# A state space branch with y and z on feature partitions, heads paired on halves of the array's columns

## The chip, the core and the metric

The kernel runs on one core of one Trainium2 chip. The metric is device time in microseconds (us) for one execution; lower is better. TensorE (PE in the rows) multiplies matrices, with its weight loads shown apart as PEld; VectorE (DVE) and ScalarE (ACT) do elementwise work, GpSimd (POOL) a few small operations, SyncE (SP) issues the DMAs. L with a number is a line of the kernel file: of the kernel before, if nothing else is said.

## The reference

Two layers of a trunk with three branches (differential attention, latent attention "MLA", and a state space branch), a gated merge and a feed-forward network, all in float32 on 512 tokens of width 1024. The change is in the state space branch. Cut to it:

```
xs, bm, cm = split(silu(causal_conv(xbc)))         # 16 heads of 64, 4 groups, state 128
dt = softplus(dt_raw + bias);  a = -exp(a_log)
# chunks of L = 128 tokens, 4 heads share a group's bm and cm
cs = cumsum(dt * a) over the chunk
decay = exp(cs[l] - cs[s]) where s <= l
y_diag = (cm[l] . bm[s] * decay) @ (xs * dt)
states = bm^T @ (xs * dt * exp(cs_end - cs));  prev = scan over chunks
y_off  = (cm @ prev) * exp(cs)
ys = (y_diag + y_off + d * xs) * silu(z)
ys = ys * rsqrt(mean(ys^2 over the group's 256 features) + eps) * ssm_norm
merged += sigmoid(gate_c) * (ys @ w_branch_c)
```

## The kernel before

**Products.** Every float32 product is made of three float32r passes: an operand is split into a high and a low part (`wh`/`wl` for weights, `hh`/`hl` for the normed input, `yh`/`yl` for a branch's result), and high x high, low x high and high x low are summed in PSUM. `mm3` (L144 to L147) issues the three. `lin_feat` (`feat_groups`) makes a product with features on partitions: per group of 256 columns two PSUM banks `mb` of 128x512, in two halves of 24 matmuls of 512 moving columns. `lin_tok` (`tok_groups`, L224 to L226) makes one with tokens on partitions: per group of 256 columns 96 matmuls of 256 moving columns. Before each half, `split` turns a loaded 128x1024 tile `wr` into `wh` (ScalarE, L140) and `wl` (VectorE, L141); three such pairs are in flight. What is plain float32 (transposes, the products inside the branch) is issued by TensorE as two instructions per matmul, except transposes.

**The branch.** `mix` runs the state space branch first, in four groups g of four heads. A group has three products: x and (b, c), each followed by a causal convolution of the bank (`conv`: one ScalarE pass L877, three VectorE taps L879 into a tile `u`, a tanh L883 and a multiply L884 into `cv`), and z. Then, on float32 operands:

- x (two 128-row tiles `cv[0]`, `cv[1]`) is transposed to tokens (L914); VectorE makes `xdt` (L918) and starts `y` with d times x (L920). b is transposed (L926), c.b is formed (L931) and masked (`cb`, L933); `xte` (L938), the states (L944) and `prev` (L946 to L951) follow.
- For each of four heads a matmul with `sel` spreads the running sum over 512 columns (L957), VectorE takes a minimum (L959), ScalarE four exponentials of 128x128 (L962), VectorE multiplies by `cb` (L963), and four matmuls with `dec` as weights and 64 columns of `xdt` moving (L965) give y with tokens on partitions.
- Three matmuls of 256 columns (L971) give the part from earlier chunks, which VectorE scales and adds (L973, L976); L968 adds the first part, L977 multiplies by silu(z).
- ScalarE sums the squares per token (L981), GpSimd takes the power -0.5 (L110).
- The `tail` of a group is issued inside the next group's products: VectorE scales y (L986), TensorE transposes it back to features (eight transposes, L990), ScalarE and VectorE split it into `yh` and `yl` (L993, L994).

After the fourth group come the gate products of the merge and its tail, then the MLA attention: its first products (L1082, L1104), VectorE's norms of them (L1088 to L1116, with four powers on GpSimd), and the transposes of `qn` and `kn` (L1123).

**What sets the order.** A scheduler lays out the instructions of each engine up to the attention; from there on TensorE's order is the one in which the code is written, and between its steps `fill` puts whole passes of waiting products (`MLA_HEAD` gives 5.737 and 2.613 us of them around the first transposes). Each engine works its queue in order, so an instruction that waits holds all that stand behind it. PSUM has four banks `mb` and four `ab`.

Of the kernel before, what the change touches and what calls it, by code (L numbers as in the profile page):

```python
# [9 lines left out]
F32 = mybir.dt.float32  # L10
# [8 lines left out]
P = 128  # L19
# [46 lines left out]
def trunk_kernel(ctx: ExitStack, tc: tile.TileContext, a: dict, out: bass.AP):  # L66
# [679 lines left out]
    def mix(l, x, hh, hl, ckr, cq, latp, scope):  # L746
# [79 lines left out]
        scratch = ssd.tile([P, 256], F32, name="yo", bufs=2).rearrange("p (i t h) -> p i t h", i=4, t=T)  # L826
# [15 lines left out]
        nc.vector.tensor_tensor(out=da, in0=dt, in1=rv["a"].unsqueeze(1).broadcast_to([P, T, SSM_H]), op=ALU.mult)  # L842
        zeros = ssd.tile([P, S], F32, name="cb")
# [3 lines left out]
        cs, ncs, tot, ecs, te = (ssd.tile([P, T, SSM_H], F32, name=nm) for nm in ("cs", "ncs", "tot", "ecs", "te"))  # L847

        def decays():

            cp = abank()
            daf = da.rearrange("p t h -> p (t h)")
            nc.tensor.matmul(cp[:, 0:n16], tri, daf, start=True, stop=True)
            nc.tensor.matmul(cp[:, n16:2 * n16], ones, daf, start=True, stop=True)
            ct = abank()
            for c in range(T):
                nc.tensor.matmul(ct[0:SSM_H, c * P:(c + 1) * P], da[:, c], tri, start=True, stop=True)
            nc.scalar.activation(cs_r[0:SSM_H], ct[0:SSM_H], AF.Copy)
            nc.vector.tensor_tensor(out=cs_r[32:32 + SSM_H], in0=ct[0:SSM_H], in1=cs_r[0:SSM_H], op=ALU.subtract)
# [3 lines left out]
            nc.scalar.activation(ecs.rearrange(flat), cp[:, 0:n16], AF.Exp)  # L863
# [6 lines left out]
        with ssd_scope:  # L870
            tails = []
            for g in range(SSM_G):
# [28 lines left out]
                sz = sp.tile([P, T, 256], F32, name="sz", bufs=2)  # L901

                def ev_z(tt, bank):
                    o = sz[:, 2 * tt:2 * tt + 2]
# [5 lines left out]
                y = sp.tile([P, T, 256], F32, name="y")  # L910
                for i in range(2):
                    tp = abank()
                    for c in range(T):
                        nc.tensor.transpose(out=tp[:, c * P:(c + 1) * P], in_=cv[i][:, c * P:(c + 1) * P], identity=ident)  # L914
                    tv = tp.rearrange("p (c r d) -> p c r d", c=T, r=2)
                    hs = slice(4 * g + 2 * i, 4 * g + 2 * i + 2)
                    sl = slice(i * P, (i + 1) * P)
                    nc.vector.tensor_tensor(out=xdt[:, :, sl].rearrange("p c (r d) -> p c r d", r=2), in0=tv,  # L918
                                            in1=dt[:, :, hs].unsqueeze(3).broadcast_to([P, T, 2, SSM_HD]), op=ALU.mult)
                    nc.vector.tensor_tensor(out=y[:, :, sl].rearrange("p c (r d) -> p c r d", r=2), in0=tv,  # L920
                                            in1=rv["dvec"][:, hs].unsqueeze(1).unsqueeze(3).broadcast_to([P, T, 2, SSM_HD]),
                                            op=ALU.mult)
# [30 lines left out]
                yps = [abank().rearrange("p (c d) -> p c d", c=2) for _ in range(2)]  # L953
                for r in range(4):
                    h = 4 * g + r
                    lp_ = abank()
                    nc.tensor.matmul(lp_, sel[:, h:h + 1].broadcast_to([P, P]), cs_r, start=True, stop=True)  # L957
                    dec = sp.tile([P, T, P], F32, name="dec", bufs=3)
                    nc.vector.tensor_tensor(out=dec, in0=lp_.rearrange("p (c l) -> p c l", c=T),  # L959
                                            in1=cs[:, :, h:h + 1].broadcast_to([P, T, P]), op=ALU.min)  # L960
                    for c in range(T):
                        nc.scalar.activation(dec[:, c], dec[:, c], AF.Exp, bias=ncs[:, c, h:h + 1])  # L962
                    nc.vector.tensor_tensor(out=dec, in0=dec, in1=cb.rearrange("p (c d) -> p c d", c=T), op=ALU.mult)  # L963
                    for c in range(T):
                        nc.tensor.matmul(yps[c // 2][:, c % 2, r * SSM_HD:(r + 1) * SSM_HD], dec[:, c],  # L965
                                         xdt[:, c, r * SSM_HD:(r + 1) * SSM_HD], start=True, stop=True)
                for i in range(2):
                    nc.vector.tensor_tensor(out=y[:, 2 * i:2 * i + 2], in0=y[:, 2 * i:2 * i + 2], in1=yps[i], op=ALU.add)  # L968
                for c in range(1, T):
                    op_ = abank()  # L970
                    nc.tensor.matmul(op_[:, 0:256], cmT[:, c * P:(c + 1) * P], prev[:, c - 1], start=True, stop=True)  # L971
                    yo = sp.tile([P, 256], F32, name="yo", bufs=2)
                    nc.vector.tensor_tensor(out=yo.rearrange("p (r d) -> p r d", r=4),  # L973
                                            in0=op_[:, 0:256].rearrange("p (r d) -> p r d", r=4),
                                            in1=ecs[:, c, hd].unsqueeze(2).broadcast_to([P, 4, SSM_HD]), op=ALU.mult)
                    nc.vector.tensor_tensor(out=y[:, c], in0=y[:, c], in1=yo, op=ALU.add)  # L976
# [611 lines left out]
```

## Time and profile before

| | us |
|---|---|
| median of 3 runs | 2073.7 (2073.63 to 2075.88) |
| the profiled execution, its own time | 2072.72 |
| its span, first to last instruction | 2071.0 |
| TensorE busy in the span | 2043.1 |
| VectorE busy | 1418.6 |
| ScalarE busy | 913.8 |

The mean granted TensorE clock of the span is 0.996 of full speed. A matmul's row shows its whole time through the array; matmuls overlap, so what one costs is the distance from its start to the next one's start. The chain that ended last is 87% TensorE.

### The profile page before, as it was taken

Reading aid. Unit: us, or ns where it says so; the run is one execution under the profiler, and the core shown is the slowest. Engines: PE = TensorE matmul, PEld = TensorE weight load, DVE = VectorE, ACT = ScalarE, POOL = GpSimd, SP = SyncE. Lnnn points to the kernel's source line nnn. Section 1 sums busy time; section 2 is a strip of 40 time slices with the busy share of each in tenths; the row PEclk is TensorE's granted clock in tenths of the full one; section 3 lists DMA queues with packets and bytes.
Section 4 is the critical chain, followed back from the end, with each engine's and each line's share of the span. In section 5 each row is a group of like instructions: output and inputs, shape, how many; then the busy total and the mean of one; then the engine's idle time right before and its main releaser. Section 6 shows DMA issues by size and latency. Waiting matters only on the chain.

```text
span 2071.0 us, 30143 instructions
## 1 busy us (share of the span) xinstructions
PE 2043.1 (99%) x11469; PEld 1769.7 (85%) x11469; DVE 1418.6 (68%) x2742; ACT 913.8 (44%) x1683; POOL 137.1 (7%) x162
## 2 busy tenths in 40 slices
PE   8999999999999999999999999999999999999999
PEld 7888987789888988888898888888998898888888
DVE  7788887756876678658757888775566566553553
ACT  6744445535533454224434544454444335432441
POOL 4200011002100000000000000110020000000000
PEclk8999999999999999999999999999999999999999
DMA  8523232233445255655443223212333243323222
GB/s 268 150 69 85 78 116 90 87 108 113 152 153 169 94 187 165 196 179 166 153 141 85 79 62 89 64 48 79 93 93 93 92 133 92 102 92 102 92 92 82
DMA packets 224542, 237.20 MB, mean 115 GB/s; under 512 B 16126, under 2 KB 195742, under 8 KB 224142
## 3 DMA queue, kind: packets, MB, share of 16 engines
q1 hardware_dynamic: 221646, 232.63, 36.3%
q0 software_dynamic: 2752, 2.65, 0.5%
q8 instruction: 90, 1.47, 0.3%
q14 instruction: 54, 0.44, 0.1%
HBM read 226.30 MB, written 8.91 MB: 114 GB/s over the span
## 4 chain that ended last, share of the span: by engine, by line
PE 87%; DVE 7%; DMA 2%; POOL 2%; issue 2%; ACT 1%; SPq 0%; POOLq 0%; DVEq 0%; ACTq 0%
PE mb L145 22%; PE mb L147 21%; PE mb L146 21%; PE mb L224 3%; PE mb L226 3%; PE mb L225 3%; PE ab L965 1%; DVE wl L141 1%; PE mb L666 1%; PE ab L1140 1%; PE ab L1177 1%; DVE macc L522 1%; PE ab L1326 1%; PE ab L1082 1%; POOL r_r L110 1%
## 5 line engine op out<-in xcount | busy, mean ns | idle before, releaser
L145 PE MATMUL mb<-hh,wh 128*128 128x512 f32 (+1 forms) x1376 | 538.2, 392 | 1.8 <-DVE g L778 0.9
L147 PE MATMUL mb<-hh,wl 128*128 128x512 f32 (+1 forms) x1376 | 532.4, 387 | 0.0
L146 PE MATMUL mb<-hl,wh 128*128 128x512 f32 (+1 forms) x1376 | 531.3, 386 | 0.0
L141 DVE TENSOR_TENSOR wl<-wr,wh 128x1024 fp32r<-128x1024 f32 (+2 forms) x312 | 374.9, 1203 | 193.8 <-ACT wh L140 192.5
L140 ACT ACTIVATE wh<-wr 128x1024 fp32r<-128x1024 f32 (+2 forms) x312 | 324.7, 1042 | 338.4 <-PE mb L146 260.5
L147 PEld LDWEIGHTS mb<-hh,wl 128*128 128x128 f32 x1376 | 258.4, 188 | 51.7
L145 PEld LDWEIGHTS mb<-hh,wh 128*128 128x128 f32 x1376 | 258.3, 188 | 51.8 <-DVE g L778 1.8
L146 PEld LDWEIGHTS mb<-hl,wh 128*128 128x128 f32 x1376 | 258.8, 188 | 49.1 <-DVE hl L702 1.2
L1423 DVE SCALAR_TENSOR_TENSOR fu<-mb,vec,fu 128x510 f32<-128x510 f32 (+1 forms) x176 | 129.8, 745 | 90.5 <-ACT fu L1421 88.9
L224 PE MATMUL mb<-wh,hh 128*128 128x256 f32 x640 | 180.1, 281 | 0.0
L226 PE MATMUL mb<-wh,hl 128*128 128x256 f32 x640 | 178.6, 279 | 0.0
L225 PE MATMUL mb<-wl,hh 128*128 128x256 f32 x640 | 178.5, 279 | 0.0
L145 PE MATMUL mb<-gh,wh 128*128 128x512 f32 (+1 forms) x432 | 151.2, 350 | 0.0
L147 PE MATMUL mb<-gh,wl 128*128 128x512 f32 (+1 forms) x432 | 150.6, 349 | 0.0
L146 PE MATMUL mb<-gl,wh 128*128 128x512 f32 (+1 forms) x432 | 150.5, 348 | 0.0
L1421 ACT ACTIVATE fu<-mb,vec 128x512 f32<-128x512 f32 x88 | 67.9, 774 | 149.7 <-PE mb L147 149.7
L224 PEld LDWEIGHTS mb<-wh,hh 128*128 128x128 f32 x640 | 120.0, 188 | 1.2 <-ACT wh L140 0.4
L225 PEld LDWEIGHTS mb<-wl,hh 128*128 128x128 f32 x640 | 120.1, 188 | 0.4
L226 PEld LDWEIGHTS mb<-wh,hl 128*128 128x128 f32 x640 | 120.2, 188 | 0.0
L522 DVE SCALAR_TENSOR_TENSOR macc<-wg,c_act,macc 128x512 f32<-128x512 f32 x140 | 104.6, 747 | 20.0 <-DMA wg<-in_ada_w_dram 19.2
L145 PE MATMUL mb<-yh,wh 128*128 128x512 f32 x256 | 104.5, 408 | 0.9 <-ACT g L769 0.9
L147 PE MATMUL mb<-yh,wl 128*128 128x512 f32 x256 | 100.3, 392 | 0.0
(333 smaller groups left out, 3373.9 us busy)
## 6 DMA issues: line engine op xcount, KB each, us to landing
wr<-in_w_in_dram SPq DMA_DIRECT2D x88, 512.0 KB
wr<-in_ffn_w_up_dram SPq DMA_DIRECT2D x88, 512.0 KB
wg<-in_ada_w_dram SPq DMA_DIRECT2D x160, 256.0 KB
wr<-in_ffn_w_down_dram SPq DMA_DIRECT2D x40, 512.0 KB
wr<-in_w_in_dram SPq DMA_DIRECT2D x64, 256.0 KB
wm<-in_ada_w_dram SPq DMA_DIRECT2D x16, 512.0 KB
wr<-in_w_branch_c_dram SPq DMA_DIRECT2D x16, 512.0 KB
wr<-in_w_out_dram SPq DMA_DIRECT2D x16, 512.0 KB
```

The lines of the kernel that those rows point to most:

```text
L110: nc.gpsimd.tensor_tensor(out=r, in0=ms, in1=nhalf[:, 0:1].broadcast_to([P, n]), op=ALU.pow)
L140: nc.scalar.activation(hi, raw[:, 0:n], AF.Copy)
L141: nc.vector.tensor_tensor(out=lo, in0=raw[:, 0:n], in1=hi, op=ALU.subtract)
L145: nc.tensor.matmul(o, lh, rh, start=first, stop=False)
L146: nc.tensor.matmul(o, lh, rl, start=False, stop=False)
L147: nc.tensor.matmul(o, ll, rh, start=False, stop=last)
L224: nc.tensor.matmul(o, hh[:, kk, ts_], wh[:, sl], start=first and k == 0, stop=False)
L225: nc.tensor.matmul(o, hh[:, kk, ts_], wl[:, sl], start=False, stop=False)
L226: nc.tensor.matmul(o, hl[:, kk, ts_], wh[:, sl], start=False, stop=last and k == 3)
L522: ins = nc.vector.scalar_tensor_tensor(out=acc[0], in0=rk, scalar=c_act[:, kk:kk + 1], in1=acc[0], op0=ALU.mult, op1=ALU.add)
L1421: nc.scalar.activation(u, bank, AF.Identity, bias=v[:, V_FCB + ti:V_FCB + ti + 1], scale=tap(2))
L1423: nc.vector.scalar_tensor_tensor(out=u[:, s_:], in0=bank[:, 0:S - s_], scalar=tap(2 - s_), in1=u[:, s_:], op0=ALU.mult, op1=ALU.add)
```

## The change

In each group z and y lie with features on partitions.

- z is made by `lin_feat` like x (48 matmuls of 512 columns), into `sz` of [128, 2, 512], one buffer.
- Two heads share a tile: for a pair, `dec` is [128, 2, 512] and one VectorE pass of 1024 elements multiplies both heads by `cb`. `xdt` (64 columns of a head) is now the weight, `dec` moves with 128 columns, and the two heads of a pair write the two halves of the output's partitions. `prev` is the weight of the earlier chunks' part: three matmuls of 128 columns per pair.
- The decay exp(cs) of that part comes from the spread running sum by ScalarE (64x384 per head, into `grow`); the tile `ecs` goes. d times x is folded into the pass that adds the product (`dcol` holds d as a column).
- The squares (ScalarE) of the two tiles are added (VectorE), and the `tail` sums them over all partitions with one float32 matmul of `ones` by 512 columns. ScalarE takes a square root, VectorE its reciprocal on 128x512, two passes scale y, and the split follows without transposes. The power on GpSimd goes.

```
-                lin_tok(w_in, [(C_Z + 256 * g, 256)], hh, hl, ev_z)
+                lin_feat(w_in, (C_Z + 256 * g, C_Z + 256 * g + P), KT, h_rhs, ev_z)
...
+                for i in range(2):
+                    dec = sp.tile([P, 2, S], F32, name="dec", bufs=2)
+                    grow = sp.tile([P, S], F32, name="yo", bufs=2)
+                    for r in range(2):
+                        h = 4 * g + 2 * i + r
+                        own = slice(r * SSM_HD, (r + 1) * SSM_HD)
+                        lp_ = abank()
+                        nc.tensor.matmul(lp_, sel[:, h:h + 1].broadcast_to([P, P]), cs_r, start=True, stop=True)
...
+                        nc.scalar.activation(grow[own, P:S], lp_[own, P:S], AF.Exp)
+                        for c in range(T):
+                            nc.scalar.activation(dec[:, r, c * P:(c + 1) * P], dec[:, r, c * P:(c + 1) * P], AF.Exp, bias=ncs[:, c, h:h + 1])
+                    nc.vector.tensor_tensor(out=dec, in0=dec, in1=cb.unsqueeze(1).broadcast_to([P, 2, S]), op=ALU.mult)
+                    yp = abank()
                     for c in range(T):
...
+                            nc.tensor.matmul(yp[own, cs_], xdt[:, c, i * P + r * SSM_HD:i * P + (r + 1) * SSM_HD], dec[:, r, cs_],
+                                             start=True, stop=True)
...
+                        nc.tensor.matmul(op_[:, cs_], prev[:, c - 1, i * P:(i + 1) * P], cmT[:, cs_], start=True, stop=True)
+                    nc.vector.tensor_tensor(out=grow[:, P:S], in0=grow[:, P:S], in1=op_[:, P:S], op=ALU.mult)
+                    j = 2 * g + i
+                    nc.vector.scalar_tensor_tensor(out=y[:, i], in0=cv[i], scalar=dcol[:, j:j + 1], in1=yp, op0=ALU.mult, op1=ALU.add)
+                    nc.vector.tensor_tensor(out=y[:, i, P:S], in0=y[:, i, P:S], in1=grow[:, P:S], op=ALU.add)
+                nc.vector.scalar_tensor_tensor(out=y, in0=y, scalar=0.5, in1=sz, op0=ALU.mult, op1=ALU.mult)
...
+                    nc.scalar.activation(sq[i], y[:, i], AF.Square, scale=1.0 / 16)
+                nc.vector.tensor_tensor(out=sq[0], in0=sq[0], in1=sq[1], op=ALU.add)
+                def tail(g=g, y=y, sq=sq[0]):
+                    ssp = abank()
+                    nc.tensor.matmul(ssp, ones, sq, start=True, stop=True)
+                    rows_ = sp.tile([P, S], F32, name="u", bufs=3)
+                    nc.scalar.activation(rows_, ssp, AF.Sqrt, bias=eps_)
+                    nc.vector.reciprocal(out=rows_, in_=rows_)
                     for i in range(2):
...
+                        nc.vector.scalar_tensor_tensor(out=y[:, i], in0=y[:, i], scalar=cw, in1=rows_, op0=ALU.mult, op1=ALU.mult)
                         yh, yl = y_tiles()
...
+                        nc.scalar.activation(yh, y[:, i], AF.Copy)
+                        nc.vector.tensor_tensor(out=yl, in0=y[:, i], in1=yh, op=ALU.subtract)
```

The change moves instructions on all engines of this stage. Three places follow; the changed kernel's lines are numbered a little higher (L921 is L914 of before, L929 L926, L934 L931, L947 L944, L886 and L891 the convolution's L879 and L884, L913 the z evacuation L906, L923 `xdt`, L1053 to L1133 the attention's L1043 to L1123).

First, VectorE in the last group of layer 0, from the products of z and of the taps of (b, c) to `xte`. Before:

```order
L879 SCALAR_TENSOR_TENSOR u<-mb,vec_89,u 128x509
L141 TENSOR_TENSOR wl<-wr,wh 128x1024
L884 SCALAR_TENSOR_TENSOR cv<-cv,u 128x512
L906 SCALAR_TENSOR_TENSOR sz<-sz,mb 128x512
L918 TENSOR_TENSOR xdt<-ab,dt 128x4x128
L906 SCALAR_TENSOR_TENSOR sz<-sz,mb 128x512
L920 TENSOR_TENSOR y<-ab,dvec 128x4x128
```

Now (the two rows of L891 are `cv[2]`, which is b, and `cv[3]`, which is c):

```order
L998 RECIPROCAL u<-u 128x512
L886 SCALAR_TENSOR_TENSOR u<-mb,vec_89,u 128x511
L1001 SCALAR_TENSOR_TENSOR y<-y,vec_89,u 128x512 x2
L886 SCALAR_TENSOR_TENSOR u<-mb,vec_89,u 128x510
L1004 TENSOR_TENSOR yl<-y,yh 128x512 x2
L886 SCALAR_TENSOR_TENSOR u<-mb,vec_89,u 128x509
L886 SCALAR_TENSOR_TENSOR u<-mb,vec_89,u 128x511
L923 TENSOR_TENSOR xdt<-ab,dt 128x4x128
L886 SCALAR_TENSOR_TENSOR u<-mb,vec_89,u 128x510
L891 SCALAR_TENSOR_TENSOR cv<-cv,u 128x512
L886 SCALAR_TENSOR_TENSOR u<-mb,vec_89,u 128x509
L913 SCALAR_TENSOR_TENSOR sz<-sz,mb 128x512 x2
```

The first `xdt` (L923), which needs TensorE's transposes of x, now stands ahead of the last taps of (b, c) and of both L891; the second L891 comes behind the two z evacuations, and then the second `xdt`.

Second, TensorE in the same group, behind the product of z. Before:

```order
L914 MATMUL ab<-ident,cv 128x128 x8
L926 MATMUL ab<-ident,cv 128x128 x3
L931 MATMUL ab<-cv 128x128 x4
L145 MATMUL mb<-hh,wh 128x512
L146 MATMUL mb<-hl,wh 128x512
```

Now:

```order
L921 MATMUL ab<-ident,cv 128x128 x8
L929 MATMUL ab<-ident,cv 128x128 x3
L145 MATMUL mb<-hh,wh 128x512
L146 MATMUL mb<-hl,wh 128x512
L147 MATMUL mb<-hh,wl 128x512
L934 MATMUL ab<-cv 128x128 x4
```

L929 transposes `cv[2]` and L934 reads `cv[3]`; three passes of a gate product now stand between them, and L929 still follows L921 at once. In the group before this one 43 passes stand between the matmul of `ones` (L995) and L921.

Third, VectorE at the end of the branch in layer 0, from the multiplication by `sz` to the attention's first line. Before:

```order
L977 SCALAR_TENSOR_TENSOR y<-y,sz 128x1024
L520 TENSOR_SCALAR macc<-wg,c_act 128x512
L522 SCALAR_TENSOR_TENSOR macc<-wg,c_act,macc 128x512
L108 TENSOR_SCALAR yn_ms<-yss 128x4
L986 TENSOR_SCALAR y<-y,yn_r 128x256 x4
L141 TENSOR_TENSOR wl<-wr,wh 128x1024
L994 SCALAR_TENSOR_TENSOR yl<-ab,vec_89,yh 128x512 x2
L1043 TENSOR_TENSOR Cq<-cos,w32q 128x4x16
```

Now:

```order
L990 TENSOR_TENSOR yo<-yo 128x512
L522 SCALAR_TENSOR_TENSOR macc<-wg,c_act,macc 128x512
L998 RECIPROCAL u<-u 128x512
L141 TENSOR_TENSOR wl<-wr,wh 128x1024
L1001 SCALAR_TENSOR_TENSOR y<-y,vec_89,u 128x512 x2
L522 SCALAR_TENSOR_TENSOR macc<-wg,c_act,macc 128x512
L1004 TENSOR_TENSOR yl<-y,yh 128x512 x2
L522 SCALAR_TENSOR_TENSOR macc<-wg,c_act,macc 128x512
L1053 TENSOR_TENSOR Cq<-cos,w32q 128x4x16
```

The reciprocal and the passes that need it stand ahead of all of the attention's work on VectorE (the L520 and L522 are layer 0's modulation sums; layer 1 has none there). On TensorE 22 passes stood between the eight transposes L990 and the attention's first product L1082; now 7 (layer 0) and 11 (layer 1) stand between the matmul of `ones` and that product. The 30 passes between the attention's first products and its transposes are the same.

## Rows read from the trace of the kernel before

**Rows 1.** Page: busy time, share of the span and instructions of each engine.
```profile
PE 2043.1 (99%) x11469; PEld 1769.7 (85%) x11469; DVE 1418.6 (68%) x2742; ACT 913.8 (44%) x1683; POOL 137.1 (7%) x162
```

**Rows 2.** One group by window: us, PE, PEld, DVE, ACT, POOL busy, PEclk, DMA, GB/s.
```profile
170.61:213.96 43.35, 43.35 (x269) 38.82 (x268) 36.63 (x60) 21.02 (x44) 1.38 (x1) 1.00 0.27 74
```

**Rows 3.** Timeline of TensorE, first group: start us, us, operation [idle before].
```profile
114.78 0.28 PE L225 MATMUL mb<-wl,hh 128*128 128x256 f32 x1
...
125.97 1.03 PE L914 MATMUL ab<-ident,cv 128*128 128x128 f32 x8
...
127.17 1.06 PE L931 MATMUL ab<-cv 128*128 128x128 f32 x8
127.99 0.48 PE L145 MATMUL mb<-hh,wh 128*128 128x512 f32 x1
...
131.08 1.46 PE L944 MATMUL ab<-xte,bmt 128*128 128x256 f32 x6
132.18 0.58 PE L957 MATMUL ab<-cs_r,sel 128*128 128x512 f32 x1
...
135.80 1.00 PE L965 MATMUL ab<-xdt,dec 128*128 128x64 f32 x8
136.60 0.71 PE L957 MATMUL ab<-cs_r,sel 128*128 128x512 f32 x2
137.15 0.40 PE L145 MATMUL mb<-hh,wh 128*128 128x512 f32 x1
```

**Rows 4.** Timeline, then group, of the attention's matmuls on halves of the columns.
```profile
399.81 1.09 PE L1177 MATMUL ab<-pT,vv 128*64 128x128 f32 x16
...
L1177 PE MATMUL ab<-pT,vv 128*64 128x128 f32 x320 | 25.4, 283 | 1.2 <-DVE pT L1142 1.2
```

**Rows 5.** Groups by shape: busy us, mean ns | idle before. Reciprocals on VectorE.
```profile
L1159 DVE RECIPROCAL sums<-sums 128x1 f32<-128x1 f32 x64 | 10.2, 159 | 9.8 <-ACT sb L1158 9.8
L832 DVE RECIPROCAL yo<-yo 128x64 f32<-128x64 f32 x2 | 1.1, 554 | 0.1
```

**Rows 6.** Timeline of VectorE: passes of 512 elements back to back.
```profile
148.19 2.08 DVE L879 SCALAR_TENSOR_TENSOR u<-mb,vec,u 128x511 f32<-128x511 f32 x3
...
1273.05 1.28 DVE L959 TENSOR_TENSOR dec<-ab,cs 128x512 f32<-128x512 f32 x2
```

**Rows 7.** Timeline of VectorE at the attention's start, layers 0 and 1.
```profile
287.69 0.21 DVE L1043 TENSOR_TENSOR Cq<-cos,w32q 128x64 f32<-128x64 f32 x1
...
289.79 0.22 DVE L1060 TENSOR_TENSOR krr<-rt,rt 128x128 f32<-128x128 f32 x1
...
1297.27 0.55 DVE L1088 TENSOR_REDUCE ss<-sb 128x4 f32<-128x384 f32 x1
...
1304.52 0.29 DVE L1060 TENSOR_TENSOR qn<-rt,rt 128x128 f32<-128x128 f32 x1
...
1306.09 0.28 DVE L1116 TENSOR_TENSOR kn<-krr,r_r 128x128 f32<-128x128 f32 x1
```

**Rows 8.** Timeline of TensorE at the attention's start, layers 0 and 1.
```profile
284.49 1.23 PE L990 MATMUL ab<-ident,y 128*128 128x128 f32 x8 [0.92 <-DVE y L986]
...
290.58 1.46 PE L1082 MATMUL ab<-wm,lat 128*128 128x192 f32 x8
...
301.73 0.60 PE L1123 MATMUL ab<-ident,qn 128*96 128x128 f32 x4
...
303.18 0.42 PE L1123 MATMUL ab<-ident,kn 128*96 128x128 f32 x2 [0.63 <-DVE kn L1116]
...
1288.92 1.23 PE L990 MATMUL ab<-ident,y 128*128 128x128 f32 x8 [0.92 <-DVE y L986]
```

**Rows 9.** Windows of the start-up (columns as in Rows 2).
```profile
40.00:44.00 4.00, 1.66 (x11) 1.25 (x9) 4.00 (x10) 2.36 (x6) 2.44 (x3) 1.00 0.24 51
44.00:48.00 4.00, 3.92 (x17) 3.57 (x17) 3.93 (x13) 3.64 (x10) 2.13 (x2) 0.59 1.08 309
```

**Rows 10.** Group of ScalarE: a load of its function table.
```profile
L830 ACT ACT_TABLE_LOAD x2 | 2.6, 1283 | 0.0
```

More of the change, by code (lines that the diff above doesn't have):

```diff
@@ L842, in mix @@
         nc.vector.tensor_tensor(out=da, in0=dt, in1=rv["a"].unsqueeze(1).broadcast_to([P, T, SSM_H]), op=ALU.mult)
+        dcol_ = ssd.tile([P, 64], F32, name="dcol")
+        dcol = dcol_[:, 0:SSM_H // 2]
+        for r in range(2):
+            own = slice(r * SSM_HD, (r + 1) * SSM_HD)
+            nc.vector.tensor_copy(out=dcol[own], in_=rv["dvec"][own].rearrange("p (j r) -> p j r", r=2)[:, :, r])
+        eps_ = dcol_[:, SSM_H // 2:SSM_H // 2 + 1]
+        nc.vector.memset(eps_, EPS)
         zeros = ssd.tile([P, S], F32, name="cb")
@@ L846, in mix @@
         nc.vector.tensor_copy(out=cs_r, in_=zeros)
-        cs, ncs, tot, ecs, te = (ssd.tile([P, T, SSM_H], F32, name=nm) for nm in ("cs", "ncs", "tot", "ecs", "te"))
+        cs, ncs, tot, te = (ssd.tile([P, T, SSM_H], F32, name=nm) for nm in ("cs", "ncs", "tot", "te"))
         def decays():
@@ L899, in mix, with ev_z @@
                 bmT, cmT = cv[2], cv[3]
-                sz = sp.tile([P, T, 256], F32, name="sz", bufs=2)
-                def ev_z(tt, bank):
-                    o = sz[:, 2 * tt:2 * tt + 2]
+                sz = sp.tile([P, 2, S], F32, name="sz")
+                def ev_z(i, bank):
+                    o = sz[:, i]
                     nc.scalar.activation(o, bank, AF.Tanh, scale=0.5)
                     nc.vector.scalar_tensor_tensor(out=o, in0=o, scalar=1.0, in1=bank, op0=ALU.add, op1=ALU.mult)
-                lin_tok(w_in, [(C_Z + 256 * g, 256)], hh, hl, ev_z)
+                lin_feat(w_in, (C_Z + 256 * g, C_Z + 256 * g + P), KT, h_rhs, ev_z)
                 xdt = sp.tile([P, T, 256], F32, name="xdt")
-                y = sp.tile([P, T, 256], F32, name="y")
+                y = sp.tile([P, 2, S], F32, name="y")
                 for i in range(2):
@@ L951, in mix @@
                         nc.vector.tensor_tensor(out=prev[:, c], in0=prev[:, c], in1=stp[:, 0:256], op=ALU.add)
[L953 to L960, printed above, removed]
-                    for c in range(T):
[L962 to L966, printed above, removed]
@@ L967, in mix @@
-                for i in range(2):
[L968 to L976, printed above, removed]
@@ new lines, in mix @@
+                nc.vector.scalar_tensor_tensor(out=y, in0=y, scalar=0.5, in1=sz, op0=ALU.mult, op1=ALU.mult)
+                sq = [sp.tile([P, S], F32, name="yo", bufs=2) for _ in range(2)]
+                for i in range(2):
+                    nc.scalar.activation(sq[i], y[:, i], AF.Square, scale=1.0 / 16)
[6 more added lines that the diff above has]
+                    nc.vector.reciprocal(out=rows_, in_=rows_)
@@ L987, in tail @@
                     for i in range(2):
-                        tp = abank()
-                        for c in range(T):
-                            nc.tensor.transpose(out=tp[:, c * P:(c + 1) * P], in_=y[:, c, i * P:(i + 1) * P], identity=ident)
+                        cw = col(V_SN + 2 * g + i)
+                        nc.vector.scalar_tensor_tensor(out=y[:, i], in0=y[:, i], scalar=cw, in1=rows_, op0=ALU.mult, op1=ALU.mult)
                         yh, yl = y_tiles()
-                        cw = col(V_SN + 2 * g + i)
```

32 lines of the change are left out of this document (13 added, 19 removed).

## The prediction

> **What bounds the kernel now.** I read the engine totals first: TensorE is busy 99% of the span, VectorE 68%, ScalarE 44% [rows 1]. Then a window of one whole group of the state space branch: in 43.35 us TensorE is busy all of it, VectorE 36.6 [rows 2]. So in this stage a TensorE pass that goes is time that goes, while VectorE has only 6.7 us to spare per group, and what is late on VectorE is a wait of TensorE. Third, TensorE's timeline, where the cost of a matmul is the distance from its start to the next one's start, not its row's length [rows 3].
>
> The sum is made against the profiled execution, 2072.72 us (1.7 above its span of 2071.0); the median of the runs is 2073.7, so 1.0 is added at the end. Under about 0.2% (4.1 us) I call it the same.
>
> **A. TensorE's passes in a group (8 groups in the two layers).**
> - Pace: 13 passes of 512 columns take 127.99 to 131.08, 0.238 with the switch at their head; 0.2294 is the value with which my sum of a whole group of before comes to its measured 43.35. The 256-column passes of z take (125.97-114.78)/95 = 0.1178 [rows 3].
> - z: 96 x 0.1178 = 11.31 becomes 48 x 0.2294 = 11.01: -0.30.
> - Product of y: a head's eight instructions of 64 columns take 135.80 to 136.60, four heads 3.20 [rows 3]. Now 32 instructions of 128 columns, whose neighbours use different halves of the array. The attention has that shape: 16 such instructions in 1.09 us, of which the last is 0.283 long, (1.09-0.283)/15 = 0.054 each [rows 4]. 32 x 0.054 = 1.73: -1.47.
> - Earlier chunks: six instructions of 256 columns at (132.18-131.08)/6 = 0.183 are 1.10; twelve of 128 at (127.99-127.17)/8 = 0.1025 are 1.23 [rows 3]: +0.13.
> - Tail: eight transposes at (1.03-0.28)/7 = 0.107 are 0.86 [rows 3]; one float32 matmul of 512 columns is not in the trace. Two instructions at twice 0.183 are 0.73, with a switch 0.83; bounds 0.69 and 0.95. I take 0.86: no change.
> - Switches between float32 and float32r: two passes around one L957 take 136.60 to 137.15 = 0.55 where two at the pace take 0.46: 0.09 to 0.10 a switch [rows 3]. By the order about ten per group become six: -0.38.
>
> Together -2.0 per group, -16.2 in all.
>
> Besides TensorE: VectorE gets the reciprocal and loses passes (d times x, the earlier chunks' scaling, four scalings), net some +2.3 per group with the reciprocal at 3.4 (below), so 38.9 of 41.3 us, 94%. ScalarE gets two table loads and the exponentials of `grow`, some +4, to 25 of 41: not a bound. From a pair's `sel` to its matmuls stand 24 to 27 passes (5.5 to 6.2 us); two minima, eight exponentials and one 1024-element multiplication need 5.0 to 5.6. I cost this and the evacuations at nothing in the six other groups; the cover is only 0.3 to 0.6 us.
>
> **B. The last group of each layer.** In the order of VectorE (first place) the first `xdt` stands ahead of the last taps and of `cv[2]`, `cv[3]`. It waits for L921, of which the start is 43 passes and 0.95 after the matmul of `ones`, 10.8 us; VectorE reaches it at about 10.0, since the reciprocal, two scalings, two splits and five taps have then run. Then: four transposes 0.43 and about 0.25 for the result to land, `xdt` 0.60, a tap 0.69 (three in 2.08) [rows 6], `cv[2]` 0.60, landing 0.09: 2.64 after L921's start. TensorE is at L929 after 0.88, and waits 1.76. Then a tap, two evacuations of z and `cv[3]`, 0.66+1.20+0.60 = 2.46, against TensorE's L929 and three passes, 0.33+0.09+0.69 = 1.11: 1.35 more, at L934. 3.1 per layer, **+6.2**. Bounds 0 and 8; if the reciprocal is short, VectorE arrives earlier and waits just the same, so this does not hang on it.
>
> **C. The start of the attention.** Here the reciprocal decides. Of 128x512 it is not in the trace: 128x1 takes 159 ns, 128x64 554 [rows 5], so 6.27 ns per element and 159+511 x 6.27 = 3.36 us. An ordinary pass of 512 is 0.60 to 0.64 [rows 6]: bounds 0.6 and 3.4. I take 3.36, as a long one in the rows.
>
> From the start of `ones` in layer 0: matmul and landing 1.1, square root 0.6 (a ScalarE pass of 512), reciprocal to 5.1, L141 to 6.2, two scalings to 7.4, a modulation pass 0.67, two splits to 9.25, another 0.67 to 9.9; then the thirteen small operations (287.69 to 289.93, 2.24) to 12.2 [rows 7]. The norms take 7.5 to `qn` (1297.27 to 1304.81) and 9.1 to `kn` (to 1306.37) [rows 7], and 0.9 more from two pieces that now stand ahead in the queues of VectorE and GpSimd: `qn` 20.6, `kn` 22.2. TensorE: 0.95, seven passes 1.6, the first products and their fill 11.15 (290.58 to 301.73) [rows 8]: 13.7. It waits 6.9, and 0.9 for `kn`, 7.8. Before it waited 0.92 at L990 and 0.63 at `kn` [rows 8]. Net +6.25. Layer 1: no modulation passes (-1.34), an L141 whose `wh` is late (+0.65), eleven passes instead of seven (-0.9): 6.2 against 0.92 [rows 8], +5.3. Together **+11.5**. Bounds: with the short reciprocal 2.7 less each, +6; with a wait of every piece +14.
>
> **D. The clock.** In the start-up TensorE was busy 1.66 of 4 us, and in the next 4 us it was busy 3.92 at a granted clock of 0.59 [rows 9]: part of it at 1.2 instead of 2.4 GHz. That is 0.41 x 4 = 1.6 us lost. A wait of 6 to 7 us is longer than that idle time, so I charge 1.65 per layer: **+3.3** (bounds 0 and, if the waits of B do it too, 6.6). The Trainium skill, "TensorE: Matmul & The Clock Gate", Part 1, says the throttled state is the default and that activity lifts it, so idle time brings it back; the trace agrees (0.59 after the idle stretch). By the page alone there would be no other sum.
>
> **Sum**: 2072.7 - 16.2 + 6.2 + 11.5 + 3.3 = 2077.5, and 1.0 to the median: **2078.5**.
>
> **Rivals.**
> 1. Faster: the waits are smaller than the passes saved. With the short reciprocal C is 6.1 and without a fall of the clock D is 0: 2072.7-16.2+6.2+6.1+1.0 = 2069.8; with half of B 2066.7; with nothing late anywhere 2057.5. For it: every term of A is read from rows. Against it: 6.27 ns per element stands in rows 5, and the second place of the chain (C) has 6.9 us of wait to lose. 0.25.
> 2. The same: B and C as forecast but no fall of the clock, 2075.2, or somewhat shorter chains, 2070 to 2077. 0.28.
> 3. Slower in every group: VectorE at 94% lets an evacuation or a tap be late, and the bank is not free. The cover is 0.3 to 0.6 us; from a delay of that size on it decides, and 1 us more in each of the eight groups gives 2086.5. Against it: VectorE's queue refills over a group, 2.4 us of slack. 0.14, part of slower.
> 4. The halves do not run side by side: 32 x 0.1025 = 3.28 where 3.20 was, so 1.5 per group comes back, 2090.9. Rows 4 speak against it: 0.054 is half of 0.1025. 0.03, part of slower.
> 5. A table load that drains ScalarE. In this trace a load takes 1283 ns with 0.0 idle before it [rows 10], so I charged no more; the load before the square root lies in ScalarE's own wait for TensorE, and the one behind it delays L140 by its length, which the 1.14 of L141 absorbs in part. If each load cost as much again, the attention's chain in each layer would end 1.35 later: 2081.2. 0.05, part of slower. The Trainium skill, "ScalarE: Activation LUTs", section "What ACT_TABLE_LOAD costs", says just that: about 1283 ns for the load and 1380 for a drain at each change of set, so square roots between exponentials are to be batched. The load agrees with rows 10; the drain does not show there.
>
> **Chances and range.** The forecast itself (2077.8 and above, up to 2083) 0.25, rivals 3 to 5 0.22 together: slower 0.47; same 0.28; faster 0.25. The range holds 8 in 10: below, half of rival 1's chance lies between 2062 and 2069.6, and half of rival 4 and the worst of 3 are left out above 2088.
>
> **What would show it.** Right: in the fourth group of each layer waits of TensorE at L929 and L934 of 1.8 and 1.3; at the attention's first transposes (L1133) some 7.8 and 6.2 us of waits, with a granted clock near 0.5 right after; L998 at 3.4 us; sixteen y matmuls of a pair in some 0.9 us; the other groups 41.3 us long. Wrong: L998 near 0.6; no wait at L929; groups still of 43 us, or idle TensorE ahead of `sel`, L934 or the first pass on a fresh bank in the groups that I took as covered.

## The result, and the profile after

| | before | changed | ratio, 95% interval |
|---|---|---|---|
| first comparison (before 4 runs, changed 4) | 2074.8 | 2101.2 | 1.012 (1.0101 to 1.014) |
| second comparison (15 and 5) | 2073.7 | 2094.3 | 1.0101 (1.0085 to 1.0116) |

The forecast was 2078.5, with 2062 to 2088 as its range. The changed kernel is slower by 1.0 to 1.2%, 21 to 26 us instead of 5: the sign was right, the size was not, and the time lies outside the range.

TensorE's work changed little (page of the changed kernel, span 2099.0 us; before stands in [rows 1]):

```profile
PE 2045.2 (97%) x11085; PEld 1742.5 (83%) x11085; DVE 1435.6 (68%) x2692; ACT 950.8 (45%) x1689; POOL 128.3 (6%) x154
```

It is busy about as long as before, in a span that is 28 us longer. That is waiting, and work done at a lower clock (mean granted clock 0.988 where it was 0.996). The waits of TensorE, grouped by what ended them (us in total, times, longest), in the profile of the changed kernel's second comparison, span 2092.5:

```profile
PE ab L1092 <- DMA wm<-in_mla_w_uq_dram: 17.0, 2, 9.6
...
PE ab L929 <- DVE cv L891: 3.2, 2, 1.6
PE ab L934 <- DVE cv L891: 2.4, 2, 1.2
...
PE mb L145 <- DVE yl L1355: 1.7, 1, 1.7
```

The second and third rows were forecast (1.76 and 1.35 a layer; measured 1.60 and 1.21). The first was not: TensorE waits at the attention's first product for a load of its weights `wm`, not at the transposes of `qn` for VectorE. The fourth has nothing to do with the branch. Where the first wait stands (timeline of TensorE, first profile, layer 0; against [rows 8]):

```profile
292.03 1.05 PE L995 MATMUL ab<-yo,ones 128*128 128x512 f32 x2
...
294.32 0.40 PE L147 MATMUL mb<-hh,wl 128*128 128x512 f32 x1
304.36 2.90 PE L1092 MATMUL ab<-wm,lat 128*128 128x192 f32 x8 [9.65 <-DMA wm<-in_mla_w_uq_dram]
...
317.46 0.60 PE L1133 MATMUL ab<-ident,qn 128*96 128x128 f32 x4
```

VectorE in the same stretch:

```profile
288.28 1.22 DVE L986 SCALAR_TENSOR_TENSOR y<-y,sz 128x1024 f32<-128x1024 f32 x1
...
293.84 3.35 DVE L998 RECIPROCAL u<-u 128x512 f32<-128x512 f32 x1 [1.28 <-ACT u L997]
297.19 1.22 DVE L141 TENSOR_TENSOR wl<-wr,wh 128x1024 fp32r<-128x1024 f32 x1
298.33 1.41 DVE L1001 SCALAR_TENSOR_TENSOR y<-y,vec,u 128x512 f32<-128x512 f32 x2
299.65 0.74 DVE L522 SCALAR_TENSOR_TENSOR macc<-wg,c_act,macc 128x512 f32<-128x512 f32 x1
```

And SyncE's DMA queue, which works in order:

```profile
290.66 0.38 SPq L123 DMA_DIRECT2D wr<-in_w_in_dram  x1
291.32 1.59 SPq L512 DMA_DIRECT2D wg<-in_ada_w_dram  x2
298.44 0.38 SPq L123 DMA_DIRECT2D wr<-in_w_in_dram  x1
300.42 0.33 SPq L512 DMA_DIRECT2D wg<-in_ada_w_dram  x1
300.84 0.39 SPq L1078 DMA_DIRECT2D wm<-in_mla_w_uq_dram  x1
```

Read from below: `wm` is issued at 300.84, right behind a `wg` that has to wait for a buffer that L522 frees (299.65 + 0.74 = 300.39). That `wg` stands behind a `wr` issued at 298.44, whose buffer L141 frees (297.19 + 1.22 = 298.41). And L141 stands behind the reciprocal. So 3.35 us on VectorE hold a queue, and the queue holds a load that needs nothing of VectorE's norm. Nothing else holds it that long: in the runs below that issue `wm` from GpSimd's queue, it goes 0.61 to 0.65 us behind the end of L986, and here L986 ends at 289.50. Layer 1 has no `wg`: there `wm` is issued at 1311.93, right behind two `wr`, of which L141 frees the second at 1311.48. Before, the same load stood in layer 0 ahead of the `wr`, right behind the two `wg`:

```profile
281.37 1.13 SPq L512 DMA_DIRECT2D wg<-in_ada_w_dram  x2
282.54 0.43 SPq L1068 DMA_DIRECT2D wm<-in_mla_w_uq_dram  x1
...
286.38 0.38 SPq L123 DMA_DIRECT2D wr<-in_w_in_dram  x1
```

The clock (windows, columns as in [rows 2]; the granted clock stands behind the five engines), first profile: at the start-up, in the fourth group, behind the attention's wait in both layers, and behind the wait for `yl`.

```profile
88.00:90.00 2.00, 2.00 (x6) 1.85 (x7) 2.00 (x3) 0.00 (x0) 0.00 (x0) 0.50 0.55 132
264.00:266.00 2.00, 2.00 (x9) 1.81 (x9) 1.84 (x3) 0.00 (x0) 0.00 (x0) 0.50 0.00 0
306.00:308.00 2.00, 2.00 (x7) 1.82 (x7) 0.18 (x1) 0.49 (x1) 0.00 (x0) 0.50 0.00 1
...
1318.00:1320.00 2.00, 2.00 (x7) 1.82 (x6) 0.29 (x1) 0.49 (x1) 0.00 (x0) 0.50 0.00 0
1640.00:1642.00 2.00, 2.00 (x6) 1.53 (x5) 0.00 (x0) 0.00 (x0) 0.00 (x0) 0.50 0.23 78
```

TensorE works at 1.2 instead of 2.4 GHz at these five places (besides two stretches of the start-up, about 28 to 38 and 45 to 49 us, that before has too), not at two. The same two waits of 1.60 and 1.21 brought the half rate in layer 0 and not in layer 1.

A group, 174.22 to 216.22 us (against [rows 2]), and its new passes:

```profile
174.22:216.22 42.00, 41.84 (x220) 34.26 (x219) 35.70 (x51) 24.03 (x44) 0.00 (x0) 1.00 0.23 63
```
```profile
185.92 1.09 PE L976 MATMUL ab<-dec,xdt 128*64 128x128 f32 x16
186.94 0.94 PE L981 MATMUL ab<-cv,prev 128*128 128x128 f32 x6
187.63 0.70 PE L964 MATMUL ab<-cs_r,sel 128*128 128x512 f32 x2
```

The period is 42.0, where 43.35 was and 41.35 was forecast. VectorE is busy 35.7 of this one, but some of the group's VectorE passes fall beyond the window's edges: the periods on either side show 37.9 and 38.5. On average of the three it is busy 37.4 of 42.5, a little more than before (36.75 of 43.8); I had it at 38.9 of 41.35.

### The profile page after: what moved, and what is told of

The parts are those of the page before. It is cut to its first block, busy times and chain, and to the rows that moved or that the text cites. A ratio compares the mean times of both kernels' runs of the same rounds, so it can differ in the third digit from the quotient of the medians.

```text
span 2099.0 us, 29317 instructions
## 1 busy us (share of the span) xinstructions
PE 2045.2 (97%) x11085; PEld 1742.5 (83%) x11085; DVE 1435.6 (68%) x2692; ACT 950.8 (45%) x1689; POOL 128.3 (6%) x154
## 5 line engine op out<-in xcount | busy, mean ns | idle before, releaser
L145 PE MATMUL mb<-hh,wh 128*128 128x512 f32 (+1 forms) x1504 | 587.4, 391 | 3.0 <-DVE g L778 1.1
L146 PE MATMUL mb<-hl,wh 128*128 128x512 f32 (+1 forms) x1504 | 581.4, 387 | 0.0
L147 PE MATMUL mb<-hh,wl 128*128 128x512 f32 (+1 forms) x1504 | 581.1, 386 | 0.0
L141 DVE TENSOR_TENSOR wl<-wr,wh 128x1024 fp32r<-128x1024 f32 (+2 forms) x312 | 375.2, 1204 | 188.1 <-ACT wh L140 186.3
L145 PEld LDWEIGHTS mb<-hh,wh 128*128 128x128 f32 x1504 | 282.5, 188 | 61.3 <-DVE g L778 2.0
L147 PEld LDWEIGHTS mb<-hh,wl 128*128 128x128 f32 x1504 | 282.7, 188 | 58.6 <-issue 1.4
L145 PE MATMUL mb<-gh,wh 128*128 128x512 f32 (+1 forms) x432 | 151.2, 350 | 0.0
L522 DVE SCALAR_TENSOR_TENSOR macc<-wg,c_act,macc 128x512 f32<-128x512 f32 x140 | 104.7, 748 | 20.4 <-DMA wg<-in_ada_w_dram 19.7
L224 PE MATMUL mb<-wh,hh 128*128 128x256 f32 x384 | 108.3, 282 | 0.0
L145 PE MATMUL mb<-yh,wh 128*128 128x512 f32 x256 | 105.3, 411 | 2.9 <-DVE yl L1355 1.7
L225 PE MATMUL mb<-wl,hh 128*128 128x256 f32 x384 | 107.1, 279 | 0.0
L226 PE MATMUL mb<-wh,hl 128*128 128x256 f32 x384 | 107.0, 279 | 0.0
L146 PE MATMUL mb<-yl,wh 128*128 128x512 f32 x256 | 100.5, 392 | 0.0
L146 PEld LDWEIGHTS mb<-gl,wh 128*128 128x128 f32 x432 | 81.5, 189 | 10.6
L145 PEld LDWEIGHTS mb<-gh,wh 128*128 128x128 f32 x432 | 81.1, 188 | 10.7
```

Of the source, the lines that this page charges most:

```text
L141: nc.vector.tensor_tensor(out=lo, in0=raw[:, 0:n], in1=hi, op=ALU.subtract)
L145: nc.tensor.matmul(o, lh, rh, start=first, stop=False)
L146: nc.tensor.matmul(o, lh, rl, start=False, stop=False)
L147: nc.tensor.matmul(o, ll, rh, start=False, stop=last)
L224: nc.tensor.matmul(o, hh[:, kk, ts_], wh[:, sl], start=first and k == 0, stop=False)
L225: nc.tensor.matmul(o, hh[:, kk, ts_], wl[:, sl], start=False, stop=False)
```

## The experiments

Besides the totals I compare stages between fixed points of TensorE's order (the first transposes of each group, the attention's first product, its first transposes, the start of the second attention), since the start-up alone differs by several us from profile to profile. "Stage X" below is the stretch from the fourth group's transposes of x to the second attention. Against before, the changed kernel's stage X is longer by 13.7 us in layer 0 and 12.1 in layer 1.

**1. The load on another queue.**
```
-                nc.sync.dma_start(out=raw[:, 0:384]...)
+                queue = nc.gpsimd if pr == 0 else nc.sync
+                queue.dma_start(out=raw[:, 0:384]...)      # and the second half alike
```


> The changed kernel, with the first load of the attention's weights (wm) of each layer issued from GpSimd's DMA queue instead of SyncE's, where it stands behind loads whose buffers VectorE frees only after the reciprocal. Theory (the load is late, but VectorE's norms are late too): TensorE's 9.65 and 7.60 us at the first product (L1092) go, and waits of about 7.5 and 5.5 us come at the first transposes; some 4.5 us less in each layer, the clock included: about 2092. Rival (the late load is the whole price): no wait in its place, 17 us of waits and 4.7 of half clock behind them go: about 2079. Other rival (the load is not held by the queue): no change, 2101.

Measured 2090.3, ratio 1.008 (1.0067 to 1.0093). The wait at the first product is gone, and others came at the first transposes (timeline of TensorE):

```profile
289.99 1.46 PE L1093 MATMUL ab<-wm,lat 128*128 128x192 f32 x8
...
303.51 0.42 PE L1134 MATMUL ab<-ident,qn 128*96 128x128 f32 x2 [1.76 <-DVE qn L1070]
308.01 0.66 PE L1134 MATMUL ab<-ident,qn 128*96 128x128 f32 x2 [4.08 <-DVE qn L1070]
...
309.58 0.66 PE L1134 MATMUL ab<-ident,kn 128*96 128x128 f32 x2 [0.47 <-DVE kn L1127]
```

6.3 us where I forecast 7.8, with half clock behind them; in layer 1 4.8 (0.21, 4.08 and 0.47) where I forecast 6.2. Stage X fell by 2.1 and 2.3 only, half of what I expected; the rival's 11 a layer is out. That the total came near the expected 2092 is luck: of its 10.9 us against the first comparison 4.4 lie in these stages. The late load is the wait that ended last, and right behind it stood the one that the prediction had.

**2. No reciprocal.** `nc.vector.reciprocal(out=rows_, in_=rows_)` is deleted.

> The changed kernel without the reciprocal (the scaling multiplies by the square root instead, so y is scaled wrongly). The order of VectorE in the last group changes with it: cv[2] and cv[3] stand ahead of xdt again. Theory (the reciprocal delays VectorE, and with it the loads on SyncE): no waits at L929 and L934 (-5.6), the attention's waits of 9.65 and 7.60 shorter by 4 to 6 each, and less half clock (-4): about 2081. Rival (the late load has nothing to do with the reciprocal): only 5.6 less, 2095.

Measured 2074.4, ratio 0.9994 (0.9985 to 1.0002): 6 to 7 below what I expected. Stage X is +3.2 and -0.4 against before, 10.5 and 12.4 less than in the changed kernel. Both waits of the fourth group are gone (VectorE's order changed back), and the load's wait is 3.25 and 0.82.

**3. Both edits.**

> Both edits: the first wm load on GpSimd's queue and no reciprocal. Theory: TensorE waits only for the norms, 4.3 and 2.9 us at the first transposes instead of 9.65 and 7.60 at the first product, no waits in the last group: about 2080, little below the kernel without the reciprocal alone. Rival (load the whole price): no wait left at the attention's start, about 2073.

Measured 2074.8, ratio 1.0001 (0.9992 to 1.0009): near the rival's number, but not by its reason, since waits are left. No wait at the first product, but 4.08 and 0.88 at the first transposes of layer 0, and half clock behind them; stage X +5.9 and -0.7. Without the reciprocal the early load wins nothing: in layer 0 it even costs, since one wait of 3.25 at the first product is cheaper than 4.96 at the transposes.

**4. Passes in the wait.**
```
             mla_load(0)
+            warm = abank()
+            for n_ in range((38, 30)[l]):
+                nc.tensor.matmul(warm, hh[:, 0, 0:P], hh[:, 0], start=True, stop=True)
```


> The changed kernel with 38 (layer 0) and 30 (layer 1) extra passes of 512 columns, whose result nothing reads, ahead of the attention's first product: 8.7 and 6.9 us of work within waits of 9.65 and 7.60. Theory (the wait brings TensorE to half clock, which costs 1.9 and 2.8 us behind it): 4.7 us less, about 2096.5. Rival (the clock falls for another reason, or the work at half clock lies beside a wait anyway): same, 2101, or more by what of the passes sticks out.

Measured 2087.3, ratio 1.0064 (1.0052 to 1.0077). The passes kept the clock up (timeline, then windows):

```profile
289.81 8.79 PE L1227 MATMUL ab<-hh 128*128 128x512 f32 x38
299.67 1.54 PE L1092 MATMUL ab<-wm,lat 128*128 128x192 f32 x8 [1.07 <-DMA wm<-in_mla_w_uq_dram]
```
```profile
299.00:301.00 2.00, 1.33 (x8) 1.36 (x9) 0.73 (x3) 0.00 (x0) 0.61 (x1) 1.00 0.52 159
1310.00:1312.00 2.00, 2.00 (x13) 1.92 (x12) 1.14 (x3) 1.08 (x3) 0.70 (x1) 1.00 0.03 8
```

Stage X fell by 1.9 and 3.1 with 68 passes more, 5.0 us. In layer 1 0.4 of it lie ahead of the first product; behind it the clock cost 1.9 and 2.8, as expected. The total fell by 7.0 against the changed kernel's second comparison: the wait of 1.75 us for `yl` in layer 1 was gone too. Run 8 is on that.

**5. The changed kernel again.**

> The changed kernel once more, unaltered. In its first profile TensorE reached the first transposes of x 4.8 us later than before, of which 3 us were half clock behind a wait of 2.15 us at 86 us; the same instructions took 0.2 to 0.4 us more than before in the two edited kernels that kept the reciprocal. Theory (that stretch varies from run to run and is not the change's): first transposes within 1 us of 126 to 127, total about 2096. Rival (the change delays the start-up by its earlier load of dvec): 130 to 131 again, total 2101.

Measured 2094.3. The first transposes come at 126.1: the 4.8 us of the first profile are not the change's. In the thirteen profiles of the changed kernel and its variants that point lies between 125.0 and 132.4.

**6. One table function for root and reciprocal.**
```
-                    nc.scalar.activation(rows_, ssp, AF.Sqrt, bias=eps_)
-                    nc.vector.reciprocal(out=rows_, in_=rows_)
+                    nc.scalar.activation(rows_, ssp, AF.Abs_reciprocal_sqrt, bias=eps_)
```


> The changed kernel with one ScalarE pass of the table function Abs_reciprocal_sqrt in place of the square root and VectorE's reciprocal. Theory (the reciprocal's 3.36 us on VectorE are the price): like the kernel without the reciprocal, 2073 to 2076, no waits at L929 and L934, 1 to 3 us at the attention's first product. Rival (the time follows the length of the norm's chain, not VectorE): 2085 or more.

Measured 2073.4, ratio 0.9997 (0.9988 to 1.0006), as run 2. On SyncE's queue `wm` now stands ahead of the `wr`:

```profile
284.09 1.11 SPq L512 DMA_DIRECT2D wg<-in_ada_w_dram  x2
285.26 0.42 SPq L1077 DMA_DIRECT2D wm<-in_mla_w_uq_dram  x1
...
292.73 0.38 SPq L123 DMA_DIRECT2D wr<-in_w_in_dram  x1
```

**7. Logarithm and exponential.**
```
+                    nc.scalar.activation(rows_, ssp, AF.Ln, bias=eps_)
+                    nc.scalar.activation(rows_, rows_, AF.Exp, scale=-0.5)
```


> The changed kernel with a logarithm and an exponential on ScalarE (two passes of 512 and a table load between or behind them) in place of square root and reciprocal: the chain from the sum of squares to the factor keeps some 2 us where the reciprocal had 3.4, but they lie on ScalarE, and VectorE is free. Theory (VectorE's place is the price): about 2075 to 2078, within 3 of the kernel without the reciprocal. Rival (the length of the chain is the price): about 2088, since 2 of 3.4 us remain.

Measured 2088.7, ratio 1.0067 (1.0055 to 1.008). My theory fell, and the rival's number came. VectorE has no reciprocal here, but it works in order, and stands idle at the scaling until the exponential is done; the L141 behind it frees the same `wr` buffer, and `wm` stands behind that `wr` again (VectorE, then SyncE):

```profile
291.07 1.41 DVE L1001 SCALAR_TENSOR_TENSOR y<-y,vec,u 128x512 f32<-128x512 f32 x2 [3.71 <-ACT u L998]
292.50 1.23 DVE L141 TENSOR_TENSOR wl<-wr,wh 128x1024 fp32r<-128x1024 f32 x1
```
```profile
293.76 0.38 SPq L123 DMA_DIRECT2D wr<-in_w_in_dram  x1
294.19 0.50 SPq L1078 DMA_DIRECT2D wm<-in_mla_w_uq_dram  x1
```

TensorE waits 8.76 and 7.69 for it. From the start of the matmul of `ones` to the first scaling (layer 0) it takes 6.30 us in the changed kernel, 4.31 here and 2.74 in run 6: run 7 is 1.6 us longer there than run 6 and costs 15 us more, with `wm` behind the `wr` instead of ahead of it. So the price is not VectorE's busy time but when the chain from the sum of squares ends, and which load stands behind it on SyncE. The waits of the fourth group shrank to 0.5 us at L934, but VectorE's order changed here too: the first `xdt` stands behind both L891.

**8. One more bank.**
```
             mla_load(0)
+            nc.tensor.matmul(abank(), hh[:, 0, 0:P], hh[:, 0], start=True, stop=True)
```


> The changed kernel with one more bank taken in each layer, by a single pass of 512 columns ahead of the attention's first product, whose result nothing reads. In the kernel with 38 and 30 such passes the wait of 1.75 us (L145 for yl of L1355, layer 1, at 1638 us) and the half clock behind it were gone. Theory (the rotation of the banks decides which earlier tile a later product's bank must wait for, and the change takes another number of them): that wait goes, layer 1 shorter by 3.5 us between the second attention and its feed-forward network, all else equal: 3.5 less than the changed kernel in the same runs. Rival (it went because of the clock or of the other passes): no change.

Measured 2095.3, ratio 1.0103 (1.0088 to 1.0119): no gain in the total. In the stage the theory holds: from the last transposes of the second attention to the feed-forward network layer 1 takes as long as before (-0.06), where the changed kernel takes 1.9 to 3.6 more, and this row of its first profile has no counterpart:

```profile
1638.00 0.51 PE L145 MATMUL mb<-yh,wh 128*128 128x512 f32 x1 [1.75 <-DVE yl L1355]
```

That pass writes a bank whose previous tile L1355 has just read; with one bank more or less the rotation gives it another. That reason is inferred, but the runs speak for it: the layer-1 wait stands in all seven profiles without the extra bank (the changed kernel's two, runs 1, 2, 3, 6 and 7) and in none of the six with one, and in run 12 it came in layer 0 instead (1.87 us at 629 us). What was won was lost at other places of that profile, which is of the slowest of the four runs (2100.2): the start-up (+2.6 against before), stage X (1.7 more than the changed kernel's first profile in layer 0, 1.4 in layer 1), a longer wait for `g` in layer 0. In stage X the half clock behind the waits of 1.60 and 1.20 lasted twice as long in layer 0 (6.8 us instead of 3.4), and it came in layer 1 too.

**9 to 12. Better versions**, all on run 6, and all with one more bank (a matmul of one column). Run 9 also has the load on GpSimd's queue and 5.2 us more passes ahead of the first transposes of layer 0; run 10 the load; run 11 nothing else; run 12 2.6 us of passes.
```
+            nc.tensor.matmul(abank()[:, 0:1], ones, ones[:, 0:1], start=True, stop=True)   # all four
-            fill(MLA_HEAD[0])
+            fill(MLA_HEAD[0] + (5.2, 0.0)[l])                                             # run 9; 2.6 in run 12
```


> The kernel with Abs_reciprocal_sqrt, and three edits: the first wm load of each layer on GpSimd's queue, 5.2 us more passes of the merge's products ahead of the first transposes of layer 0 (taken from those that follow later), and one more bank in each layer (a matmul of one column). Theory: no wait at the first product, the 4 to 5 us wait for qn of layer 0 lies under the passes, the wait for yl in layer 1 goes: 2073.4 - 4.8 - 1.9 = about 2067, faster than before by 0.3%. Rival (the passes are missed later in the attention, or their weights' splits delay the norms on VectorE): 2070 to 2073.

> Abs_reciprocal_sqrt, the first wm load on GpSimd's queue and one more bank. Theory (behind the late load stands the wait for the norms): the 2.9 us at the first product of layer 0 go and some 4 us come at qn with half clock behind them; only the bank's 1.9 in layer 1 and the 0.5 at layer 1's first product are won: 2071 to 2073. Rival (the load was the last wait): 2068.

> Abs_reciprocal_sqrt and one more bank in each layer (a matmul of one column). Theory: the wait of 1.75 us for yl in layer 1 goes, 1.9 less: 2071.5. Rival (another product's bank then waits): 2073.4.

> Abs_reciprocal_sqrt, one more bank, and 2.6 us more passes ahead of the first transposes of layer 0; the wm load stays on SyncE's queue. Theory (the load's wait stands ahead of these passes and is not covered by them): the 2.9 us at the first product stay, only the 0.7 at kn goes: 2071. Rival (all waits of that place are one budget): 2068.5.

| run | us | ratio, interval | stage X, layers 0 and 1 |
|---|---|---|---|
| 9 | 2072.0 | 0.9992 (0.9983 to 1.0001) | +4.2, -0.7 |
| 10 | 2071.7 | 0.9991 (0.9982 to 0.9999) | +4.6, -0.7 |
| 11 | 2069.5 | 0.998 (0.9971 to 0.999) | +2.7, -0.7 |
| 12 | 2081.3 | 1.0032 (1.002 to 1.0045) | +7.9, -0.5 |

Run 11 is faster than before, by 4.5 us; 1.9 less than run 6 was expected, 3.9 came (the start-up of its profile alone is 2.3 shorter than run 6's). Its waits of TensorE in the rebuilt stages are these, none above 3.0:

```profile
PE ab L1091 <- DMA wm<-in_mla_w_uq_dram: 3.4, 2, 3.0
...
PE ab L1132 <- DVE kn L1125: 0.5, 1, 0.5
```

Run 10 came as expected. In run 9 the rival's number came: the moved passes themselves wait (4.46 us, L145 for VectorE's L775), since their own products' results have to be evacuated on the VectorE that is late. In run 12 neither number came (2071 and 2068.5 expected, 2081.3 measured): the load's wait stays (2.84), the passes are missed later in layer 0, in waits of 0.2 to 2.1, and the wait for `yl` came in layer 0, with half clock behind it.

## Why the prediction was wrong

The forecast added 4.8 us to the profile of before, and the second profile of the changed kernel (span 2092.5, the start-up within 0.2 of before) has 21.5 more. Its terms against that profile:

| step | forecast | measured | how measured |
|---|---|---|---|
| A, passes of eight groups | -16.2 | -10.4 | six periods shorter by 1.30 on average, times 8 (the fourth groups taken like the others) |
| B, fourth groups | +6.2 | +5.6 | waits at L929, L934 |
| C, attention's start | +11.5 | +14.5 | 9.58 + 7.40 at L1092, less 0.92 and 0.63, and 0.92, of before [rows 8] |
| D, clock | +3.3 | +6.3 | run 4: 4.7 behind C; 1.6 behind B of layer 0 |
| not forecast: the bank of L145 in layer 1 | 0 | +1.9 | run 8 |

They sum to 17.9 of 21.5. The rest I did not follow up: 1.8 of it lie inside the two stages X, 1.3 between the second attention of layer 0 and layer 1's first group.

So the largest step that failed, by price, is A's sum of passes (5.8 too much saved); then the place of the wait in C and the number of falls in D (3.0 each) and a bank that was not in the sum (1.9). The late load alone did not take the time out of the range: without it (run 1) the kernel still measured 2090.3.

- **C had the wrong wait.** The reciprocal was worked out at 3.36 and is 3.35 long; VectorE's delay is as forecast (from the start of `ones` to the first small operation 10.15, forecast 9.9). But I followed it only along VectorE's own line to `qn`. The step that failed is "the first products and their fill 11.15" in TensorE's line: it lets the first product start at once, and puts its load `wm` at nothing, without a reason. I did not ask which buffers the late L141 and L522 free, and what stands behind those loads on SyncE's queue. The load's wait (17.0 in the two layers) took the place of the norms' (14.0 forecast). That the sizes are near is in part luck: with the load out of the way (run 1) the norms' waits were 11.1. Run 7 speaks for the queue's order as what decides, not the reciprocal as such; a kernel that keeps the reciprocal and has `wm` ahead of the `wr` on SyncE's own queue was not run.
- **A was too large by 0.7 per group.** Here the step was the estimates for shapes that the trace did not show in this use. Sixteen instructions of y go from 185.92 to 186.94, 0.064 each where the attention's row gave 0.054 [rows 4]: 0.3. The earlier chunks' six take 0.69, 0.115 each where I had 0.1025: 0.15. And the eight transposes L990 that went had taken 0.71 (198.76 to 198.90 and 199.90 to 200.47 in before), where I had 0.86: 0.15. Together these are 0.6; some 0.1 is a wait of TensorE for `dec` (0.16 at 193.97). The two terms that rest on L944, another shape, stood. Two of before's L971, and the matmul of `ones`, with the pass behind them:
```profile
184.50 0.59 PE L971 MATMUL ab<-prev,cv 128*128 128x256 f32 x2
184.75 0.58 PE L145 MATMUL mb<-hh,wh 128*128 128x512 f32 x1
185.16 1.00 PE L965 MATMUL ab<-xdt,dec 128*128 128x64 f32 x8
```
```profile
203.08 1.02 PE L995 MATMUL ab<-yo,ones 128*128 128x512 f32 x2
203.54 0.80 PE L145 MATMUL mb<-hh,wh 128*128 128x512 f32 x1
204.18 0.39 PE L146 MATMUL mb<-hl,wh 128*128 128x512 f32 x1
```
  The distance to the next start shows only a part of the price: the pass behind them takes 0.41 and 0.64 instead of 0.23. With that, the two L971 cost 0.43, 0.17 each and a switch (I had 0.183 and a switch), and `ones` 0.87 (I had 0.86).
- **B stood as forecast**, to 0.16 us at either place. That it does not hang on the reciprocal is not shown by a run: in runs 2, 6 and 7 the order of VectorE changed with it, and the waits went (run 7 keeps 0.5 at L934). The trace speaks for it: VectorE reached the first `xdt` 0.94 us ahead of L921's result (1.5 by the forecast's terms), so with this order a shorter reciprocal would not have shortened the waits.
```profile
258.95 0.69 DVE L923 TENSOR_TENSOR xdt<-ab,dt 128x512 f32<-128x512 f32 x1 [0.94 <-PE ab L921]
```
- **D had the price about right and the places wrong**: 1.65 for one fall was forecast, 1.6 to 2.8 measured (run 4 and the windows), but instead of two there were three falls in the second profile (not counting the start-up) and five in the first. The step that failed is "1.65 per layer", at the attention alone; the fall behind B stood only in its bounds.
- **The table load's rival** did not come. The Trainium skill, "ScalarE: Activation LUTs", section "What ACT_TABLE_LOAD costs", puts a drain of about 1380 ns beside the load of about 1283 at every switch to another set. Here the load agrees (1.28), and the drain does not show. Between the root's end and L769's start lies the load's 1.28 alone, here as in [rows 10] (timeline of ScalarE, changed kernel):
```profile
293.12 0.69 ACT L997 ACTIVATE u<-ab,dcol 128x512 f32<-128x512 f32 x1 [1.07 <-PE ab L995]
293.83 1.28 ACT L769 ACT_TABLE_LOAD   x1
295.12 1.09 ACT L769 ACTIVATE g<-mb 128x512 f32<-128x512 f32 x2
```
- **Two more rivals fell.** The halves of the array do run side by side (0.064 against 0.115), each beside its neighbour. And VectorE, which I had at 94%, is not late in every group: it is busy 37.4 of 42.5 (88%), and the groups between have no wait above 0.2.

What I should have seen: in the trace of before the first `wm` is issued 0.04 us behind a `wg`, and the `wr` comes after it. Which loads stand ahead of it in the changed kernel was a question to ask before pricing the first product.

## What to carry to other kernels

A longer step on an engine that works in order delays everything that stands behind it there, and through the buffers that these later steps free also the DMA queue, with loads on it that have nothing to do with the step: follow each of them to the engine that waits. When one wait is taken away, price the next one before counting the gain (run 1: 17 us of wait gone, 4.4 won in those stages). And a matmul's price can stand in the pass behind it: take the distance to the start after that. A change of how many tiles a rotating pool hands out can make a stage far behind it wait; one tile more may cure it (run 11) or move the wait elsewhere (run 12).

## What the runs showed of the hardware

- A reciprocal on VectorE costs by the element: 3.35 us for 512 columns, 0.554 for 64 and 0.159 for one [rows 5], where another pass of 512 takes 0.6 to 0.75. ScalarE's `Abs_reciprocal_sqrt` did root and reciprocal of the same tile in one pass of 0.69.
- 68 passes whose result nothing reads made the two stages X shorter by 5.0 us; 4.7 of it lie behind the wait, where TensorE was at 2.4 GHz and not at 1.2 (run 4).
- The same gaps, 1.60 and 1.21 us, lowered the clock in layer 0 and left it in layer 1, in both profiles of the changed kernel; in run 8, with the same gaps, it fell in both layers.
